# Experts' input: the split parts stored in the order of x, the gather reading every eighth column as its weights

## Chip, cores and metric

The kernel runs on one core of a Trainium2 chip. The metric is the device time of one execution in microseconds (us). Engines are named as in the profile: PE is TensorE's matmul side and PEld its weight loads, DVE is VectorE, ACT is ScalarE, POOL is GpSimd, SP is SyncE, whose queue issues the loads of the weights.

## What is computed

The reference chains a block of two layers (gated linear attention and spatial gating, cross attention to a memory, a mixture of 16 experts) and a second block of one layer (attention and a state space mixer, then again a mixture of 16 experts). All data is float32: 256 tokens of 1024 features. The change lies in the mixture of experts, which thus runs three times. Per layer it is

```python
h = jax.nn.silu(xt @ w_gate[e]) * (xt @ w_up[e])        # for each expert e of 16
y = y + gate[:, e:e + 1] * (h @ w_down[e])              # gate: 2 of the 16 experts per token
```

with `xt` of 256 x 1024, `w_gate[e]` and `w_up[e]` of 1024 x 512, `w_down[e]` of 512 x 1024, so 96 MB of expert weights per layer and 288 MB in all.

## The kernel before

Tokens lie on the partitions in two tiles of 128 (`tt` = 0, 1). In front of each mixture of experts, `before_moe` (line 329) takes the output of the last projection, normalises it and computes the router's logits `lg`. It also prepares the experts' input. `normal` (line 346) scales the rows on ACT into `z`; `high` (line 353) copies `z` on ACT to a tile `xsh` of type float32r, its high part; `low` (line 357) subtracts on DVE and writes the rest to `xsl`. The four views that these steps use come from `views` (line 341). In the trace these are `xsh<-x` (`xsh<-h` in the third layer) at L98, the line of the helper `cp`, and `xsl<-x,xsh` at L78, the line of the helper `tt`.

The order of columns matters here. The expert weights are loaded (line 206) with rows that follow each other on a partition, partition p holding rows 8p to 8p+7, so that a tile of the contraction needs features p*8+k for a fixed k. The kernel before brings the input into that order when it splits it: `high` and `low` read `z` as "p (j k) -> p k j", every eighth element first, 32 bytes apart, and write `xsh` and `xsl` so that feature 8j+k stands at column 128k+j. Tile k is then 128 neighbouring columns.

`moe` (line 848) runs the router, which ends in `sel` and `pos`, the slot of each token at each of its experts. `Dm` (L78) holds ones where a token belongs to a slot, 64 slots per expert. `gather` (line 872) multiplies with it: `lhsT`, the weights that PE loads, is a tile of 128 columns of `xsh` or `xsl`; the moving operand is `Dm` for four experts, 256 columns. For one pair of tiles k that is 2 parts x 2 tiles k x 2 token tiles, 8 weight loads and 8 matmuls; the results go from PSUM to `XG` through ACT and DVE (lines 92, 91, 95). All matmuls are issued in the helper at L64, so that they are told apart by tile names: `gath` is the gather, `gu` the gate and up products, `dn` the down product, `ysum` the sum into the output.

Per layer the first four experts are gathered at once before any expert product, 32 matmuls of `gath`. The further 12 experts come in 12 bursts of 8, two in each of the first six turns of the loop over expert pairs, in the order of the program: gate product, `ysum` of two pairs before, burst, up product, down product of the pair before, burst. So there are 128 `gath` matmuls per layer, 384 in all, and 12 splits of 128 x 1024 (six `high`, six `low`).

The expert weights arrive in loads of 1 MB. Some 17 are issued before the experts begin (`preload`, line 193), into rooms that other stages use otherwise; each further load goes into a room that an earlier one leaves, and SP waits in its queue until the product that reads the earlier one (`gu` or `dn` on PE) is done.

Of the kernel before, what the change touches and what calls it, by code (L numbers as in the profile page):

```python
# [17 lines left out]
KT = D // 128  # L18
# [6 lines left out]
class Net:  # L25
# [303 lines left out]
    def before_moe(self, x, rw, v, mean, keep, got):  # L329

        nc = self.nc
        w, G, B, n = rw
        xs = [self.t8(i, None, F32R) for i in ("xsh", "xsl")]
        lg = self.sm("lg", [128, 40], bufs=1)[:, :2 * n].rearrange("p (t n) -> p t n", t=2)
        mv, q, st, rs, nr = {}, {}, {}, {}, {}

        def views(tt):
            z = x[:, tt, :] if mean else keep[:, tt, :]
            return [z] + [z.rearrange("p (j k) -> p k j", k=KT)] + \
                [i[:, tt, :].rearrange("p (k j) -> p k j", k=KT) for i in xs]

        def normal(tt):
            z = views(tt)[0]
            if mean:
                self.act(z, x[:, tt, :], AF.Identity, scale=rs[tt], bias=nr[tt])
            else:  # L350
                self.act(z, x[:, tt, :], AF.Copy, scale=rs[tt])

        def high(tt):
            _, z, h, _ = views(tt)
            return self.cp(h, z).ins

        def low(tt):
            _, z, h, o = views(tt)
            self.tt(o, z, h.bitcast(F32), OP.subtract)

        def finish(tt):

            self.mul(x[:, tt, :], x[:, tt, :], v[:, 0, :])
            self.add(x[:, tt, :], x[:, tt, :], v[:, 1, :])

        def part(tt, c, A):
            with self.urgent("bm"):
                return steps(tt, c, A)

        def steps(tt, c, A):  # L370
            o = x[:, tt, c * 512:(c + 1) * 512]
            if c == 0:
                st[tt] = self.sm("st", [128, 2, 6])
                q[tt] = self.acc([128, n], "q")
            if mean:
                self.stt(o, o, ALPHA, A, OP.mult, OP.add)
            else:
                self.stt(o, A, 0.5, o, OP.mult, OP.add)
            z = self.s2("zT", [128, 4, 128])
            p = self.rp([128, 4, 128], "trp")  # L380
            for j in range(4):
                kk = 4 * c + j
                nc.tensor.transpose(p[:, j, :], x[:, tt, kk * 128:(kk + 1) * 128], self.ident)
            self.cp(z, p)
            if mean:
                nc.vector.bn_stats(st[tt][:, c, :], o)
            for j in range(4):
                kk = 4 * c + j
                turned = self.mm(q[tt], z[:, j, :], w[:, kk, :], kk == 0, kk == KT - 1).ins
            if c == 0:  # L390
                if tt:
                    normal(0)
                    high(0)
                    low(0)
                return
            rs[tt] = self.sm("rs", [128, 1])
            if mean:
                mv[tt] = self.sm("mv", [128, 2])
                nc.vector.bn_aggr(mv[tt], st[tt])
                self.rsqrt(rs[tt], mv[tt][:, 1:2], 1e-5, near=True)  # L400
            else:
                ss = self.sm("ss", [128, 1])
                self.act(xs[1][:, tt, :], x[:, tt, :], AF.Square, scale=0.03125, accum_out=ss)
                self.rsqrt(rs[tt], ss, 1e-6, near=True)
            p = q[tt]
            if mean:
                g = self.sm("lgt", [128, n])
                self.stt(g, G, mv[tt][:, 0:1], p, OP.mult, OP.add)
                p = g
                nr[tt] = self.sm("nr", [128, 1])  # L410
                self.stt(nr[tt], mv[tt][:, 0:1], -1.0, rs[tt], OP.mult, OP.mult)
            self.stt(lg[:, tt, :], p, rs[tt], B, OP.mult, OP.add)
            if tt == 0:
                return turned
            normal(1)

        def second(exp):
            with self.after(exp):
                h = high(1)
            if exp:  # L420
                with self.after(h):
                    self.warm()
        got.extend((lg, xs, (second, lambda: low(1)), (lambda: [finish(t) for t in range(2)]) if mean else None))
        return part
# [423 lines left out]
    def moe(self, lg, xs, second, finish, gc, route, Wg, Wu, Wd, fill, source):  # L848
# [14 lines left out]
        Dm = self.t8("Dm", [128, 2, 16, 64], F32R)  # L863
# [8 lines left out]
        def gather(e, ks):  # L872

            if e >= NE:
                return
            if e not in XG:
                XG[e] = self.t8("XG", [128, KT, 4, 64])
            with self.urgent("ga"):
                ps = {k: self.rp([128, 2, 4, 64], "gath") for k in ks}
                for i in range(2):  # L880
                    for k, p in ps.items():
                        for kk in (k, k + 1):
                            for tt in range(2):
                                self.mmp(p[:, kk - k], xs[i][:, tt, kk * 128:(kk + 1) * 128], Dm[:, tt, e:e + 4, :],
                                         tt == 0 and i == 0 and kk == k, tt == 1 and i == 1)
                for k, p in ps.items():
                    for kk in (k, k + 1):
                        o, g = XG[e][:, kk], gain[:, kk:kk + 1]
                        b = None if offset is None else offset[:, kk:kk + 1]
                        if kk % 2:  # L890
                            last = self.ts(o, p[:, kk - k], g, b, OP.mult, None if b is None else OP.add)
                        else:
                            self.act(o, p[:, kk - k], AF.Copy if b is None else AF.Identity, scale=g,
                                     **({} if b is None else {"bias": b}))
            return last
# [3 lines left out]
        with self.after(first):  # L899
            second[1]()  # L900
        last = gather(0, (0, 2, 4, 6))
        with self.after(first):
            for e in (4, 8, 12):
# [107 lines left out]
        for i in range(NE // 2):  # L1011
            pg = up(i, 0)
            if i > 1:
                spread(i - 2)
            gather(i // 2 * 4 + 4, (4 * (i % 2),))
            pu = up(i, 1)
            h = middle(pg, pu)
            if i:
                down(i - 1)
            gather(i // 2 * 4 + 4, (4 * (i % 2) + 2,))  # L1020
            if i == 0:
                slot_gates()
            if i == last and over:
                self.tc.keep_in_program_order(
                    nc.vector.tensor_scalar(flag, cm, float(self.cap), None, op0=OP.is_gt))
            rows(i)
            fill(i)
            turned(i, h)
# [515 lines left out]
```

## Time and profile before

| | us |
|---|---|
| median of 3 runs | 1460.03 |
| lowest and highest of them | 1458.52, 3515.89 |
| the profiled execution, its own time | 1460.11 |
| its span, first to last instruction | 1458.3 |
| busy in the span: PE | 1375.7 |
| busy in the span: PEld | 899.7 |
| busy in the span: DVE | 636.3 |
| busy in the span: ACT | 504.8 |

The profile is of one execution. What lies around the span is 1460.11 - 1458.3 = 1.8 us. PEld runs beside PE, so their sum is no time. Matmuls are pipelined: the busy time of one, some 0.28 us for 256 columns, is longer than the step from one to the next, which has to be read from how many fit in a stretch. Times of the three mixtures of experts in the span: 258 to 480 us, 700 to 920 us, 1193 to 1410 us.

### The profile page before, as it was taken

To read this page: it belongs to the slowest core of one execution; us is meant where nothing else is said; L and a number is where in the kernel's file an instruction comes from. 1 tells how busy PE (TensorE), PEld (TensorE's weight loads), DVE (VectorE), ACT (ScalarE), POOL (GpSimd) and SP (SyncE) were. 2 spreads that over 40 slices of the span, in tenths; PEclk is the share of its full clock that TensorE was granted. 3 is DMA by queue.
4 is the path that set the end of the run, shared out by engine and by line. 5 is a ranking of instruction groups with operands and counts; after the bars stand their busy time and mean duration, and the time that the engine had idled before them with its cause. 6 is when DMAs were issued, how large, how long until landed. Compare 5 with 4: busy or idle time off the path is not lost. (4 is left out here: it accounts for less than half of the span.)

```text
span 1458.3 us, 18050 instructions
## 1 busy us (share of the span) xinstructions
PE 1375.7 (94%) x7258; PEld 899.7 (62%) x7258; DVE 636.3 (44%) x1088; ACT 504.8 (35%) x784; POOL 63.7 (4%) x107
## 2 busy tenths in 40 slices
PE   8999999999988898999899998799999979999987
PEld 7889897444433686898444433499878864444335
DVE  5754754412111767654512111657776641212134
ACT  5634443211101474443211101548764440111132
POOL 2110000000000103000000000000000000000000
PEclk9999999999999999999899999899999989999998
DMA  9745557799999965446799999844534679999991
GB/s 341 271 173 173 174 178 267 280 399 421 420 419 420 320 224 175 145 174 243 297 404 380 422 420 420 326 133 134 185 129 137 227 288 378 421 380 420 420 380 44
DMA packets 101964, 421.50 MB, mean 289 GB/s; under 512 B 10676, under 2 KB 10896, under 8 KB 65008
## 3 DMA queue, kind: packets, MB, share of 16 engines
q1 hardware_dynamic: 97968, 409.17, 72.4%
q0 software_dynamic: 3904, 11.09, 2.3%
q8 instruction: 60, 0.98, 0.3%
q14 instruction: 32, 0.26, 0.0%
HBM read 419.18 MB, written 1.05 MB: 288 GB/s over the span
## 5 line engine op out<-in xcount | busy, mean ns | idle before, releaser
L64 PE MATMUL gu<-we,XG 128*64 128x512 f32 x1536 | 347.0, 596 | 4.2 <-DMA we<-in_w_up_dram 1.9
L78 DVE TENSOR_TENSOR whl<-raw,whl 128x1024 fp32r<-128x1024 f32 (+1 forms) x210 | 241.1, 1163 | 144.6 <-ACT whl L98 143.7
L98 ACT ACTIVATE whl<-raw 128x1024 fp32r<-128x1024 f32 (+1 forms) x210 | 208.2, 1009 | 200.8 <-PE acc L64 97.2
L64 PEld LDWEIGHTS gu<-we,XG 128*64 128x64 f32 x1536 | 108.1, 137 | 208.2 <-issue 193.9
L64 PE MATMUL acc<-whl,xTh 128*128 128x512 f32 (+2 forms) x640 | 193.0, 387 | 4.6 <-ACT xTh L98 3.4
L64 PE MATMUL dn<-we,mid 128*64 128x512 f32 x768 | 179.3, 599 | 16.0 <-DMA we<-in_w_down_dram 13.9
L64 PEld LDWEIGHTS dn<-we,mid 128*64 128x64 f32 x768 | 58.0, 138 | 130.2 <-issue 101.6
L64 PEld LDWEIGHTS acc<-whl,xTh 128*128 128x128 f32 x640 | 119.6, 194 | 29.9 <-ACT xTh L98 4.0
L64 PE MATMUL facc<-xTh,whl 128*128 128x256 f32 x640 | 123.8, 289 | 1.7 <-ACT xTh L98 1.7
L64 PE MATMUL acc<-whl,xTl 128*128 128x512 f32 (+1 forms) x320 | 119.8, 385 | 0.2 <-DVE xTl L78 0.2
L95 ACT ACTIVATE dh<-dn,gsl 128x512 fp32r<-128x512 f32 x42 | 28.9, 688 | 258.8 <-PE dn L64 258.8
L78 DVE TENSOR_TENSOR mid<-mid,gu 128x512 f32<-128x512 f32 x24 | 25.3, 1056 | 211.3 <-PE gu L64 138.7
L64 PEld LDWEIGHTS facc<-xTh,whl 128*128 128x128 f32 x640 | 103.2, 195 | 2.4 <-ACT xTh L98 1.9
L64 PE MATMUL facc<-xTl,whl 128*128 128x256 f32 x320 | 91.6, 287 | 0.0
L87 DVE SCALAR_TENSOR_TENSOR dl<-dn,gsl,dh 128x512 fp32r<-128x512 f32 x42 | 31.5, 750 | 127.6 <-ACT dh L95 125.2
L95 ACT ACTIVATE XG<-gath,gc 128x256 f32<-128x256 f32 x48 | 25.3, 535 | 125.8 <-PE gath L64 117.8
L64 PEld LDWEIGHTS acc<-whl,xTl 128*128 128x128 f32 x320 | 60.5, 193 | 12.7 <-issue 0.7
L64 PEld LDWEIGHTS facc<-xTl,whl 128*128 128x128 f32 x320 | 61.9, 193 | 0.5 <-issue 0.3
L92 DVE TENSOR_SCALAR XG<-gath,gc 128x256 f32<-128x256 f32 x32 | 17.1, 543 | 100.6 <-ACT XG L95 100.2
L95 ACT ACTIVATE mid<-gu 128x512 f32<-128x512 f32 x24 | 14.3, 595 | 121.9 <-PE gu L64 115.4
L64 PE MATMUL acc<-whl,oTh 128*128 128x512 f32 x160 | 49.5, 402 | 0.5 <-ACT oTh L98 0.5
L64 PEld LDWEIGHTS gath<-Dm,xsh 128*128 128x128 f32 x192 | 30.7, 221 | 27.0 <-issue 17.1
(366 smaller groups left out, 1759.3 us busy)
## 6 DMA issues: line engine op xcount, KB each, us to landing
we<-in_w_gate_dram SPq DMA_DIRECT2D x96, 1024.0 KB, 12.7
we<-in_w_up_dram SPq DMA_DIRECT2D x96, 1024.0 KB, 11.8
we<-in_w_down_dram SPq DMA_DIRECT2D x96, 1024.0 KB, 16.7
raw<-in_w_in_dram SPq DMA_DIRECT2D x38, 1024.0 KB, 10.2
raw<-in_w_out_dram SPq DMA_DIRECT2D x12, 1024.0 KB, 5.0
raw<-in_wk_x_dram SPq DMA_DIRECT2D x8, 1024.0 KB, 9.1
raw<-in_wv_x_dram SPq DMA_DIRECT2D x8, 1024.0 KB, 5.7
raw<-in_wq_x_dram SPq DMA_DIRECT2D x8, 1024.0 KB, 5.0
```

Source lines behind the costliest of these rows:

```text
L64: return self.nc.tensor.matmul(out, lhsT=l, rhs=r, start=start, stop=stop, skip_group_check=True)
L78: return self.nc.vector.tensor_tensor(out, a, b, op=op)
L87: return self.nc.vector.scalar_tensor_tensor(out, a, s, b, op0=op0, op1=op1, **k)
L92: return self.nc.vector.tensor_scalar(out, a, s1, s2, op0=op0, op1=op1)
L95: return self.nc.scalar.activation(out, a, f, **k)
L98: return self.nc.scalar.activation(out, a, AF.Copy)
```

## The change

`views` hands `high` and `low` plain rows: both read `z` and write `xsh` and `xsl` in the order of the features, contiguous on both sides. The gather picks its tile itself: its weights are now the 128 columns k, k+8, k+16, ..., that is every eighth float32 of a row, 32 bytes apart. The values and the rest of the program are the same. The order of the instructions on PE, ACT, DVE, POOL and SP, with their shapes, is the same in both kernels, row for row; only the access patterns of the 12 splits and of the 384 weight loads differ.

```diff
         def views(tt):
             z = x[:, tt, :] if mean else keep[:, tt, :]
-            return [z] + [z.rearrange("p (j k) -> p k j", k=KT)] + \
-                [i[:, tt, :].rearrange("p (k j) -> p k j", k=KT) for i in xs]
+            return [z, z] + [i[:, tt, :] for i in xs]
...
                             for tt in range(2):
-                                self.mmp(p[:, kk - k], xs[i][:, tt, kk * 128:(kk + 1) * 128], Dm[:, tt, e:e + 4, :],
+                                self.mmp(p[:, kk - k], xs[i][:, tt, :].rearrange("p (j k) -> p k j", k=KT)[:, kk], Dm[:, tt, e:e + 4, :],
                                          tt == 0 and i == 0 and kk == k, tt == 1 and i == 1)
```

## Rows read from the trace of the kernel before

**Rows 1.** Windows: us, length, busy (count) per engine, PEclk, DMA share, GB/s.
```profile
420.00:480.00 60.00, 50.83 (x227) 19.56 (x227) 10.03 (x16) 8.04 (x13) 0.00 (x0) 1.00 1.02 416
880.00:920.00 40.00, 33.36 (x135) 11.61 (x133) 4.46 (x8) 4.02 (x6) 1.05 (x2) 0.96 1.02 416
1360.00:1400.00 40.00, 36.15 (x160) 13.18 (x158) 5.15 (x7) 3.65 (x6) 0.00 (x0) 1.00 1.02 419
```
**Rows 2.** Windows around the pauses of the weight loads, columns as in rows 1.
```profile
306.00:310.00 4.00, 4.00 (x28) 2.40 (x28) 2.67 (x5) 1.65 (x3) 0.00 (x0) 1.00 0.86 313
790.00:796.00 6.00, 6.00 (x32) 2.00 (x30) 1.06 (x1) 0.00 (x0) 0.00 (x0) 1.00 0.50 172
1284.00:1290.00 6.00, 6.00 (x32) 2.00 (x30) 1.06 (x1) 0.00 (x0) 0.00 (x0) 1.00 0.49 167
```
**Rows 3.** Waits of SP's queue from 776 to 800: us in total, times, longest.
```profile
SPq L213 <- PE gu L64: 17.8, 2, 13.0
```
**Rows 4.** Splits: by tile, ns min/median/max; by form, busy us, mean ns, idle before.
```profile
L98 ACT ACTIVATE xsh<-x x4: 2026/2048/2162, 249.1 to 697.1; 128x1024 fp32r<-128x1024 f32 x4
L78 DVE TENSOR_TENSOR xsl<-x,xsh x4: 1991/2018/2034, 251.8 to 700.4; 128x1024 fp32r<-128x1024 f32 x4
...
L78 DVE TENSOR_TENSOR whl<-raw,whl 128x1024 fp32r<-128x1024 f32 x186 | 224.8, 1222 | 136.1 <-ACT whl L98 135.2
L98 ACT ACTIVATE whl<-raw 128x1024 fp32r<-128x1024 f32 x186 | 193.6, 1056 | 179.3 <-PE acc L64 87.4 <-PE facc L64 58.7 <-DMA raw<-in_w_ple_proj_dram 17.0
...
L78 DVE TENSOR_TENSOR whl<-raw,whl 128x528 fp32r<-128x528 f32 x24 | 16.3, 704 | 8.6 <-ACT whl L98 8.4
L98 ACT ACTIVATE whl<-raw 128x528 fp32r<-128x528 f32 x24 | 14.7, 640 | 21.5 <-PE acc L64 9.8 <-PE facc L64 5.9 <-DMA raw<-in_w_in_dram 4.0
```
**Rows 5.** Timeline, first layer, tile 1: start us, us, engine, line [idle before].
```profile
251.79 1.99 DVE L78 TENSOR_TENSOR xsl<-x,xsh 128x1024 fp32r<-128x1024 f32 x1
252.01 2.12 POOL L104 TENSOR_TENSOR rs<-rs,mhalf 128x1 f32<-128x1 f32 x1 [4.43 <-DVE rs L103]
254.17 0.16 DVE L87 SCALAR_TENSOR_TENSOR nr<-mv,rs 128x1 f32<-128x1 f32 x1 [0.39 <-POOL rs L104]
```
**Rows 6.** Timeline, second layer: split of tile 0 and the logits behind it.
```profile
691.92 2.05 ACT L98 ACTIVATE xsh<-x 128x1024 fp32r<-128x1024 f32 x1
694.01 2.00 DVE L78 TENSOR_TENSOR xsl<-x,xsh 128x1024 fp32r<-128x1024 f32 x1 [1.34 <-ACT xsh L98]
695.93 0.22 DVE L87 SCALAR_TENSOR_TENSOR lgt<-gwc,mv,q 128x16 f32<-128x16 f32 x1
```
**Rows 7.** Timeline, third layer: the second high part and the gather that waits.
```profile
1192.66 2.05 ACT L98 ACTIVATE xsh<-h 128x1024 fp32r<-128x1024 f32 x1
...
1194.76 3.33 PE L64 MATMUL gath<-Dm,xsh 128*128 128x256 f32 x15 [0.52 <-ACT xsh L98]
```
**Rows 8.** Weight loads: by tile, ns min/median/max; by form, busy us, mean ns.
```profile
L64 PEld LDWEIGHTS gath<-Dm,xsl x192: 187/192/330, 262.0 to 1345.7; 128*128 128x128 f32 x192
...
L64 PEld LDWEIGHTS gu<-we,XG 128*64 128x64 f32 x1536 | 108.1, 137 | 208.2 <-issue 193.9 <-DMA we<-in_w_gate_dram 5.2 <-DMA we<-in_w_up_dram 5.1
```
**Rows 9.** Timeline, first layer: second half of the first burst.
```profile
272.27 0.64 PE L64 MATMUL gath<-Dm,xsl 128*128 128x256 f32 x4
```
**Rows 10.** Windows of tile gath alone, start of each first gather (PE, PEld, DVE, ACT).
```profile
258.54:262.20 3.66, 3.63 (x16) 3.61 (x17) 0.00 (x0) 0.00 (x0) 0.50 0.16 65
700.25:706.20 5.95, 5.95 (x27) 5.90 (x28) 0.54 (x1) 0.90 (x2) 0.50 0.22 92
1193.65:1197.90 4.25, 3.69 (x16) 3.43 (x17) 0.00 (x0) 0.00 (x0) 0.53 0.69 287
```
**Rows 11.** Windows of tile gath alone, between first gather and pause of the loads.
```profile
264.50:306.00 41.50, 3.97 (x26) 3.35 (x27) 2.74 (x6) 2.19 (x5) 1.00 0.87 345
707.00:793.00 86.00, 8.29 (x56) 7.21 (x56) 4.81 (x10) 4.53 (x9) 1.00 0.92 379
1200.20:1286.00 85.80, 8.31 (x56) 7.25 (x56) 4.24 (x9) 3.64 (x8) 1.00 0.92 380
```

## Prediction

> **What bounds the kernel now.** I read the windows first, stage by stage. In the three mixtures of experts the DMA engines are full to the end: a share of 1.02 at 416 to 419 GB/s, while PE is busy in only 50.83 of 60, 33.36 of 40 and 36.15 of 40 us [rows 1]. So at the end of each layer PE waits for weights, and it has slack there of 9.2, 6.6 and 3.9 us. A mixture of experts therefore ends when its last load lands. When that is, is set by the last pause of the loads, the last time that SP stood for a room that PE had not yet left. The windows with a low DMA share show these pauses: a share of 0.86 over 4 us around 308, then 0.50 and 0.49 over 6 us around 793 and 1287, with PE busy all the time [rows 2]. The waits of SP's queue name the releaser: the product `gu` on PE, up to 13.0 us in one wait [rows 3]. What makes PE late before the pause comes out one for one at the end of the layer; what makes it late afterwards is hidden, until the slack at the end is used up. That is the frame for both parts of the change.
>
> **Part 1, the splits: a gain.** The 12 splits read every eighth element and take about 2.05 us on ACT and 2.02 us on DVE [rows 4]. The same two instructions with contiguous rows of the same length and types are the splits of the projection weights, 1.06 and 1.22 us [rows 4]. I expect these durations: 1.0 us less for each `high`, 0.8 us less for each `low`. Of 12 splits only those in front of the first gather's start count, and the timeline of each layer shows which:
> - First layer: POOL's `rs`, 0.5 to 0.6 us long elsewhere, takes 2.12 us and ends at 254.13, 0.35 us after DVE's `low` ends, and `nr` with the whole router chain follows it [rows 5]. DVE's `low` starts at 251.79 behind other work and is 0.8 us shorter; `rs` follows: gain 0.8.
> - Second layer: `high` on ACT, `low` on DVE right behind it, then `lgt`, the first step of the logits, right behind that [rows 6]. Gain 1.0 + 0.8 = 1.8.
> - Third layer: both `high` follow one another on ACT (the first, as long, starts at 1189.1), and the gather waits for the second one [rows 7]. Gain 2 x 1.0 = 2.0.
>
> Sum 4.6 us. The bounds are 0 (another wait ends last) and 12 times 0.9, some 11 us.
>
> **Part 2, the weights of the gather: a loss.** No row shows a weight load with a step, so I bound it. A contiguous load of 128 columns takes 0.19 us and one of 64 columns 0.137 [rows 8], so a column costs (0.190 - 0.137) / 64 = 0.8 ns and the 128 columns 0.10 us. A matmul of 256 columns needs as much, and both overlap: four `gath` matmuls take 0.64 us, one alone 0.28, so the step is (0.64 - 0.28) / 3 = 0.12 us [rows 9]. Lower bound of the change: nothing. For the other bound I take the engines that do read with this step. DVE's contiguous element costs (1222 - 704) / 496 = 1.04 ns, ACT's (1056 - 640) / 496 = 0.84 ns; the step adds (2018 - 1222) / 1024 = 0.78 and (2048 - 1056) / 1024 = 0.97 ns [rows 4]. So both engines, with different speeds of their own, come out at 1.8 ns per element. That looks like a price of the memory, paid per jump, and not of the engine. At 1.8 ns the load needs 128 x 1.8 = 0.23 us, covers the matmul's 0.10 and becomes the step: 0.12 -> 0.23, +0.11 us per matmul. At the granted clock of 0.50 (1.2 GHz) the step is already 3.66 / 16 = 0.23 and 5.95 / 27 = 0.22 us [rows 10], so there I add 0.02. The value I take is that one, the nearest row in kind (same step, same type, same memory).
>
> The Trainium skill (SBUF — State Buffer, Specifications) says that SBUF works in lines of 16 bytes and that an access pays when it does not hit a line at least twice. With 32 bytes between elements each is alone in its line. The slow splits agree with it; no run here shows it for TensorE, and the page gives no price.
>
> Per layer the first gather (32 matmuls) and 12 bursts of 8 pay:
> - A burst: 8 x 0.11 = 0.88 us; all 12 of a layer 10.6 us.
> - First gather, at half clock for about 16, 27 and 13 of its 32 matmuls [rows 10] (in the third, 13 at that step before the clock rises): 16 x 0.02 + 16 x 0.11 = 2.1 us; 27 x 0.02 + 5 x 0.11 = 1.1; 13 x 0.02 + 19 x 0.11 = 2.4.
> - Net with part 1, before the first `gu`: 2.1 - 0.8 = +1.3; 1.1 - 1.8 = -0.7; 2.4 - 2.0 = +0.4.
>
> **The sum.** Before the last pause lie 26, 56 and 56 `gath` matmuls [rows 11], so 3, 7 and 7 bursts, 2.6, 6.2 and 6.2 us. The shift of the last load is then 1.3 + 2.6 = 3.9; -0.7 + 6.2 = 5.5; 0.4 + 6.2 = 6.6. The other limit is PE itself: the net of the start plus 10.6 minus the slack of rows 1, that is 1.3 + 10.6 - 9.2 = 2.7; -0.7 + 10.6 - 6.6 = 3.3; 0.4 + 10.6 - 3.9 = 7.1. The larger of the two holds: 3.9 + 5.5 + 7.1 = 16.5 us. What follows a mixture of experts (sum, normalisation, transposes) hangs on its end and moves along. The profiled execution took 1460.1 us, as the median did within 0.1, so I forecast 1476.6 us, 1.1% slower. A difference of 2% (29 us) is about what a measurement of this kernel can tell from no change, so this falls under "same".
>
> **Rivals.**
> - *Weight loads do not care about the step.* Then part 1 alone is left, and since both pauses and slack move with the first `gu`: 1460.1 - 4.6 = 1455.5. For it: the load runs beside the matmul on a path of its own, and a column at 0.8 ns is slow enough that a memory with some reserve could follow. Against it: ACT contiguous needs 0.84 ns, the same pace, and yet the step doubles it. This rival is on the other side of zero; it decides as soon as the loads stay below some 0.2 us. In the same direction the Trainium skill (TensorE: Matmul & The Clock Gate, LDWEIGHTS (loading the stationary operand)) gives the duration of a load by its columns alone, 1/1.2 ns each, which agrees with the 0.8 ns here and knows no term for a step.
> - *The step costs engine cycles and not memory time*, so that loads double at half clock too, to 128 x 3.3 = 0.42 us. The half-clock matmuls then pay 0.21 in place of 0.02, (16 + 27 + 13) x 0.19 = 10.6 us more at most: up to 1487. For it: at half clock, contiguous loads do slow down (330 against 187 ns [rows 8]). Against it: the clock rises with time, so fewer matmuls fall into the slow stretch; I count 1485.
> - *The load is far dearer*, some four times (0.43 us at full clock, if it also no longer runs beside the matmul). A burst then costs 8 x 0.31 = 2.5 us, a layer 30 us and 5 to 8 for the first gather; PE becomes the bound: about 30 + 5 - 2 - 7 = 26 per layer, 1538. For it speaks only that nothing here shows such a load.
> - *All is hidden behind the loads.* Only the net at the start is left, about 1 us in sum: 1461. Against it: the slack of rows 1 is smaller than 10.6 in every layer, and two of the pauses lie late.
>
> **Chances.** Forecast 0.57, own range 1469 to 1484. First rival 0.24, second 0.08, third 0.07, hidden 0.04. The range takes in the first rival and the second and leaves out the third: 1453 to 1490, with some 0.03 below and 0.12 above. Faster by over 2% (below 1430.9): no case reaches it, 0.01. Slower by over 2% (above 1489.3): the third, a part of the second and a tail of the forecast, 0.12. Within 2%: 0.87.
>
> **What would show it.** Splits at 1.06 and 1.22 us, `rs` in the first layer near 1.3 us, `gath` loads of about 0.3 us with a step of 0.23 between matmuls of a burst (a burst in 1.9 us in place of 1.1), the pauses near 793 and 1287 some 5 us later relative to the layer's start, and less idle PE in the last 40 us of each layer. The forecast is wrong if the loads stay at 0.19 us (then 1455), or if PE shows no idle time at all at the end of a layer and DMA does (then the loads cost more than I took).

## Result and the profile after

The changed kernel takes 1479.96 us in the median of 4 runs (1476.29 to 1482.21), the kernel before 1461.6 beside it: ratio 1.0127, 95% interval 1.0107 to 1.0146, that is 15.6 to 21.3 us more. One execution of the kernel before took 3515.89 us and is left out of the ratio. A later comparison gave 1478.1 us of 6 runs and 1.0122 (1.0104 to 1.0140). The forecast was 1476.6 us, 16.5 more: the sign is right, and the size is 1 to 2 us short by the differences of the medians (18.4 and 17.6), 4 by the profiles. The profiled execution took 1480.63 us, its span is 1478.8: 20.5 more than before.

**The two parts, by instruction.** The groups by form, of the changed kernel (busy us, mean ns of one, idle before):

```profile
L64 PEld LDWEIGHTS gath<-Dm,xsl 128*128 128x128 f32 x192 | 50.2, 339 | 0.0
L78 DVE TENSOR_TENSOR xsl<-x,xsh 128x1024 fp32r<-128x1024 f32 x4 | 4.9, 1220 | 0.3 <-ACT xsh L98 0.3
L98 ACT ACTIVATE xsh<-x 128x1024 fp32r<-128x1024 f32 x4 | 4.2, 1051 | 0.0
```

The splits stand at 1.05 us (ACT) and 1.22 us (DVE), where they were 2.05 and 2.02 [rows 4]; the weight loads at 0.34 us instead of 0.19 [rows 8]. Here is the first burst in the timeline of the changed kernel, to be laid beside [rows 9] (start us, us):

```profile
272.21 1.25 PE L64 MATMUL gath<-Dm,xsh 128*128 128x256 f32 x4
273.30 1.15 PE L64 MATMUL gath<-Dm,xsl 128*128 128x256 f32 x4
274.37 1.08 PE L64 MATMUL gu<-we,XG 128*64 128x512 f32 x4
```

Four matmuls take 1.15 us where they took 0.64. From start to start of each the step is 0.240 us, against 0.120 before. Behind `gu` or `dn` the first step of a burst grows from 0.22 to 0.35, and such a burst, from the last product in front of it to the first behind it, is 0.97 to 1.02 us longer. Four bursts of each layer (the fifth, seventh, ninth and eleventh) stand behind `ysum`; there the first step stays at 0.12, and they are 0.85 to 0.88 longer. The forecast had 0.88 for all; the 12 bursts of a layer come to 11.3 us, not 10.6. At this step of 8 elements the clock does not change the time from one matmul to the next. Windows of the changed kernel over the first gather of the first layer, its first half at 0.50, its second with the clock risen:

```profile
257.00:261.00 4.00, 3.84 (x15) 3.85 (x16) 3.86 (x10) 0.23 (x1) 0.00 (x0) 0.50 0.34 141
261.00:265.00 4.00, 4.00 (x18) 4.00 (x17) 1.17 (x3) 1.69 (x3) 0.00 (x0) 0.92 0.00 0
```

and its timeline there:

```profile
257.16 4.29 PE L64 MATMUL gath<-Dm,xsh 128*128 128x256 f32 x16 [0.84 <-DVE Dm L78]
261.24 3.97 PE L64 MATMUL gath<-Dm,xsl 128*128 128x256 f32 x16
```

From start to start it is 0.240 us in both halves, but for the first two steps of 0.38 and 0.34 (and two of 0.20 and 0.23 as the clock rises). Before, it was 0.213 in the half at 0.50 and 0.118 to 0.120 at full clock.

**What the shorter splits release.** First layer, tile 1, timeline of the changed kernel, answering to [rows 5]:

```profile
251.09 1.22 DVE L78 TENSOR_TENSOR xsl<-x,xsh 128x1024 fp32r<-128x1024 f32 x1
251.32 1.40 POOL L104 TENSOR_TENSOR rs<-rs,mhalf 128x1 f32<-128x1 f32 x1 [4.43 <-DVE rs L103]
...
252.75 0.16 DVE L87 SCALAR_TENSOR_TENSOR nr<-mv,rs 128x1 f32<-128x1 f32 x1 [0.44 <-POOL rs L104]
```

POOL's `rs` begins 0.22 to 0.23 us behind the start of DVE's `xsl` in both kernels, and ends 0.41 us after it here (252.72 against 252.31), 0.35 before: 2.12 us became 1.40 without any change to POOL's instruction. In the third layer the gather waits for the second high part as before, which is now 1.04 us long; its wait is down to 0.23 us [rows 7]:

```profile
1205.43 3.99 PE L64 MATMUL gath<-Dm,xsh 128*128 128x256 f32 x15 [0.23 <-ACT xsh L98]
```

**The loads and the slack.** Windows of the changed kernel, columns as in rows 1: first the pauses, then the ends of the layers.

```profile
306.00:310.00 4.00, 4.00 (x22) 1.41 (x20) 0.00 (x0) 0.00 (x0) 0.00 (x0) 1.00 1.00 420
310.00:314.00 4.00, 4.00 (x24) 3.02 (x22) 1.98 (x3) 1.99 (x4) 0.00 (x0) 1.00 0.61 188
796.00:804.00 8.00, 8.00 (x38) 2.90 (x40) 1.02 (x2) 0.56 (x1) 0.00 (x0) 1.00 0.18 72
1302.00:1308.00 6.00, 6.00 (x30) 2.01 (x28) 0.37 (x1) 0.00 (x0) 0.00 (x0) 1.00 0.03 11
430.00:470.00 40.00, 40.00 (x184) 14.83 (x182) 4.49 (x6) 3.17 (x5) 0.00 (x0) 1.00 1.01 419
890.00:930.00 40.00, 36.30 (x154) 13.12 (x152) 6.12 (x11) 5.48 (x9) 1.05 (x2) 0.96 1.02 415
1370.00:1410.00 40.00, 39.88 (x188) 17.03 (x190) 6.97 (x11) 5.41 (x9) 0.00 (x0) 1.00 1.01 420
```

The pauses of [rows 2] are later and deeper (a share of 0.18 over 8 us around 800, 0.03 over 6 us around 1305). SP still waits for `gu`, up to 13.9 us in one wait where it was 13.0 [rows 3]. And the idle PE time in these windows [rows 1] has shrunk: none in the first layer, 3.7 us in the second, 0.1 in the third. What PE still waits for to the end of the first layer (400 to 486 us: us in total, times, longest) was before:

```profile
PE dn L64 <- DMA we<-in_w_down_dram: 5.3, 4, 1.3
PE gu L64 <- DMA we<-in_w_up_dram: 1.9, 1, 1.9
PE gu L64 <- DMA we<-in_w_gate_dram: 0.8, 1, 0.8
PE dn L64 <- ACT mid L98: 0.7, 1, 0.7
PE trp L450 <- DVE DT L91: 0.4, 1, 0.4
```

and is in the changed kernel:

```profile
PE dn L64 <- ACT mid L98: 0.7, 1, 0.7
PE trp L449 <- DVE DT L91: 0.4, 1, 0.4
```

No wait for a load is left: here PE itself has become the limit. In the third layer the full window is not the whole story, for behind it PE still waits for a load:

```profile
1419.33 1.94 PE L64 MATMUL dn<-we,mid 128*64 128x512 f32 x8 [1.35 <-DMA we<-in_w_down_dram]
```

The page says the same in its groups for the expert products (busy us, mean ns, idle before), first of the kernel before:

```profile
L64 PE MATMUL gu<-we,XG 128*64 128x512 f32 x1536 | 347.0, 596 | 4.2 <-DMA we<-in_w_up_dram 1.9 <-DMA we<-in_w_gate_dram 1.9 <-DVE XG L92 0.2
...
L64 PE MATMUL dn<-we,mid 128*64 128x512 f32 x768 | 179.3, 599 | 16.0 <-DMA we<-in_w_down_dram 13.9 <-ACT mid L98 2.1
```

and of the changed one:

```profile
L64 PE MATMUL gu<-we,XG 128*64 128x512 f32 x1536 | 343.8, 601 | 0.1
...
L64 PE MATMUL dn<-we,mid 128*64 128x512 f32 x768 | 176.0, 598 | 6.5 <-DMA we<-in_w_down_dram 4.4 <-ACT mid L98 2.1
```

PE stood idle in front of these products for 20.2 us before and for 6.6 now: 13.6 of the 34 us that the 36 bursts add went into idle time.

**One thing that was not in the forecast.** Behind the second burst of each layer the granted clock falls to 0.50 (1.2 GHz). Timeline of the changed kernel, PE, first layer, from the start of the second burst to that of the third:

```profile
281.39 1.25 PE L64 MATMUL gath<-Dm,xsh 128*128 128x256 f32 x4
...
283.46 1.84 PE L64 MATMUL pg<-gparts,Dm 128*128 128x4 f32 x16
285.16 0.82 PE L75 MATMUL dtp<-ident,pos 128*128 128x128 f32 x4
285.77 1.06 PE L75 MATMUL gut<-ident,mid 128*128 128x128 f32 x4
286.76 8.14 PE L64 MATMUL gu<-we,XG 128*64 128x512 f32 x32
294.83 1.24 PE L64 MATMUL gath<-Dm,xsh 128*128 128x256 f32 x4
```

The same stretch of the kernel before:

```profile
279.85 0.74 PE L64 MATMUL gath<-Dm,xsh 128*128 128x256 f32 x4
...
283.63 7.09 PE L64 MATMUL gu<-we,XG 128*64 128x512 f32 x32
290.65 0.74 PE L64 MATMUL gath<-Dm,xsh 128*128 128x256 f32 x4
```

and the windows of the changed kernel in the three layers:

```profile
286.00:288.00 2.00, 2.00 (x8) 0.96 (x9) 1.04 (x3) 0.60 (x1) 0.00 (x0) 0.50 0.92 385
730.00:732.00 2.00, 2.00 (x9) 1.02 (x9) 1.04 (x3) 0.60 (x1) 0.00 (x0) 0.50 0.96 401
1236.00:1238.00 2.00, 2.00 (x6) 0.48 (x4) 0.00 (x0) 0.00 (x0) 0.00 (x0) 0.54 0.13 53
```

Between the starts of the second and third burst lie 2.65 us more than before, not 1.0, so the fall costs some 1.65 us there. PE was not idle ahead of it: it did the burst, and then 16 `pg` matmuls of four columns, each behind a weight load.

**Ledger.** For each layer, the time from the start of the first `gu` to that of the last `ysum` in each kernel's profiled execution; a star marks a layer in which the clock fell behind one of its first two bursts.

| us | layer 1 | layer 2 | layer 3 |
|---|---|---|---|
| before | 220.9 | 219.7 | 220.7 |
| splits alone | 220.6 | 219.6 | 220.7 |
| changed | 223.0* | 228.1* | 229.1* |
| changed, second profile | 222.5 | 229.5* | 227.4 |
| gather alone | 223.1* | 226.1 | 230.6* |
| changed, `pg` ahead of the up product | 224.2* | 226.5 | 228.9* |
| changed, `pg` apart from bursts | 221.4 | 226.9 | 227.6 |
| the same, second profile | 221.6 | 226.7 | 227.5 |

Changed against before: layers +2.2, +8.4, +8.5, start of the first `gu` +0.5, stages between the layers -0.6 and +2.5 (in the second of them the clock falls at 1067 and 1101 in the changed kernel's profile and not in that of before, which in turn has a longer fall at 928 to 941; what these are worth is not shown), behind the last `ysum` -0.9: 20.5 in sum.

### The profile page after: what moved, and what is told of

It reads as the page before. It is cut to its first block, busy times and chain, and to the rows that moved or that the text cites. A ratio compares the mean times of both kernels' runs of the same rounds, so it can differ in the third digit from the quotient of the medians.

```text
span 1478.8 us, 18050 instructions
## 1 busy us (share of the span) xinstructions
PE 1413.9 (96%) x7258; PEld 939.4 (64%) x7258; DVE 631.9 (43%) x1088; ACT 498.8 (34%) x784; POOL 62.6 (4%) x107
## 3 DMA queue, kind: packets, MB, share of 16 engines
HBM read 419.18 MB, written 1.05 MB: 284 GB/s over the span
## 5 line engine op out<-in xcount | busy, mean ns | idle before, releaser
L64 PE MATMUL dn<-we,mid 128*64 128x512 f32 x768 | 176.0, 598 | 6.5 <-DMA we<-in_w_down_dram 4.4
L64 PEld LDWEIGHTS gath<-Dm,xsh 128*128 128x128 f32 x192 | 49.4, 332 | 24.3 <-issue 16.2
L64 PE MATMUL gath<-Dm,xsh 128*128 128x256 f32 x192 | 55.0, 424 | 3.8 <-DVE Dm L78 3.6
```

What stands on the lines that cost most here:

```text
L64: return self.nc.tensor.matmul(out, lhsT=l, rhs=r, start=start, stop=stop, skip_group_check=True)
```

## Experiments

**Each part alone.** Splits alone: the changed kernel with the weights of the gather read as before.

```diff
-xs[i][:, tt, :].rearrange("p (j k) -> p k j", k=KT)[:, kk]
+xs[i][:, tt, kk * 128:(kk + 1) * 128]
```

> Part 1 alone: the splits are contiguous as in the changed kernel, the gather loads 128 neighbouring columns as before, so the features that it gathers are in another order than the rows of the expert weights; the threshold of the fallback is raised so that its loop can't start. Theory (the two parts are independent; the loss is the weight loads, the gain is the splits): 4 to 5 us faster than before, about 1456.5; first gu about 0.8, 1.8 and 2.0 us earlier after the start of the router's stage in the three layers; weight loads of the gather at 0.19 us; no fall of the clock behind the second burst. Rival (part of the changed kernel's gain on the path was only apparent, another wait ends last): no change, 1460 to 1461.

Measured: 1453.83 us, ratio 0.995 (0.9933 to 0.9967), 4.8 to 9.8 us faster. The gain is there and rather larger than the 4.6 of the forecast. The profiled execution, the slowest of the four, is 4.3 us shorter. Counted from the router's first matmul (`q`), the first gather starts 0.7, 1.8 and 1.7 us earlier in the three layers, as forecast but for 0.3 in the third. At the first `gu`, where 0.8, 1.8 and 2.0 were expected, only 0.0, 2.2 and 1.0 are left; the remaining 1.1 us lie outside these stages. What is lost or won behind the gather's start goes with the clock: by their steps some 25, 20 and 25 of its 32 matmuls run at half clock, where it was 17, 27 and 14. In the first layer the last 16 take 2.93 us against 2.15.

Gather alone: the kernel before with the gather's line of the change, so with the diff above the other way round.

> Part 2 alone: the splits are strided as before, and the gather takes every eighth column, so again the features are in another order than the expert weights; fallback threshold raised. Theory: the changed kernel without its gain, 1480 + 4.5 = 1484.5 us, some 23 us over before; a step of 0.24 us between gather matmuls and weight loads of 0.34 us; the clock falls behind the second burst in each layer. Rival (the strided loads cost less, the changed kernel lost elsewhere): 1470 or below.

Measured: 1482.29 us, ratio 1.0155 (1.0138 to 1.0171), 20 to 25 us slower. The clock falls behind the second burst in the first and third layer, not in each as expected. So the loss is all in the strided weights; by the medians the splits give back some 4 of it (1.0155 - 1.0127 of 1461 us), about what the forecast had put for them.

**Same loads, other place.** The kernel before, with strided weights for one group of four experts only, the last (bursts 9 to 12) or the second (bursts 1 to 4): 96 strided loads in both.

```diff
-xs[i][:, tt, kk * 128:(kk + 1) * 128]
+(xs[i][:, tt, :].rearrange("p (j k) -> p k j", k=KT)[:, kk] if e == 12 else xs[i][:, tt, kk * 128:(kk + 1) * 128])
```

> Splits as before; only the gather of the last four experts (bursts 9 to 12 of each layer, behind the last pause of the weight loads) takes every eighth column, 32 of 128 matmuls per layer; features of these experts in another order, fallback threshold raised. Theory (what makes PE late behind the last pause is hidden by the loads up to the slack at the end, 9.2, 6.6 and 3.9 us): 4 x 0.98 = 3.9 us more of PE per layer, all or nearly all hidden: 1460 to 1463, within 0.2% of before. Rival (PE is the bound and each us counts wherever it lies): 3 x 3.9 = 11.8 us slower, 1473.

> Splits as before; only the gather of experts 4 to 7 (bursts 1 to 4 of each layer, ahead of the last pause) takes every eighth column, again 32 matmuls per layer; features of these experts in another order, fallback threshold raised. Theory: 3.9 us per layer lie ahead of the pause and come out at the end of the layer (3 us in the first layer), and the clock falls behind the second burst and adds up to 1.7 us per layer: 11 to 16 us slower, 1472 to 1477. Rival that all PE time is hidden by the loads: 1461. Rival that place does not matter: the same time as with the last four experts.

Measured: late 1461.65 us, ratio 1.0007 (0.9995 to 1.002); early 1474.74 us, ratio 1.007 (1.0037 to 1.0103). Twelve late bursts cost nothing measurable, twelve early ones 5 to 15 us. The five early runs spread from 1466 to 1476 us, and the profile is of the one at 1474.74. The windows show why early and late differ. Late bursts:

```profile
790.00:796.00 6.00, 6.00 (x30) 2.01 (x28) 1.06 (x1) 0.00 (x0) 0.00 (x0) 1.00 0.49 165
1360.00:1400.00 40.00, 37.75 (x176) 14.56 (x173) 5.22 (x8) 4.12 (x6) 0.00 (x0) 1.00 1.01 418
```

Early ones:

```profile
790.00:796.00 6.00, 6.00 (x32) 3.42 (x30) 0.54 (x1) 1.16 (x2) 0.00 (x0) 1.00 1.01 419
796.00:802.00 6.00, 6.00 (x30) 2.01 (x28) 0.43 (x1) 0.00 (x0) 0.00 (x0) 1.00 0.34 139
```

With the late bursts the pause stands where it stood [rows 2] and only slack is eaten: 37.75 busy of 40 us against 36.15 [rows 1]. With the early ones the pause itself is 6 us later. By the ledger's measure the layers with late bursts take 220.7, 219.5 and 220.7 us, as before. With the early ones the third layer is 3.8 us longer, for four bursts of 1.0, and the second 7.1, with a fall of the clock behind its second burst. So the mechanism of the forecast is shown for the second and third layer: what makes PE late before the last pause counts, what comes behind it is hidden up to the slack. It fails in the first layer: three of the four bursts lie ahead of its pause, 3 us, and the layer is 0.6 us longer (221.5), with PE still waiting for loads. Why the loads make up the rest there is open.

**What is paid for.** The changed kernel with steps of 2, 3, 4 and 16 elements for the weights of the four groups of experts.

```diff
-xs[i][:, tt, :].rearrange("p (j k) -> p k j", k=KT)[:, kk]
+(lambda s, f: f[:, :128 * s].rearrange("p (j k) -> p k j", k=s)[:, kk % s])((2, 3, 4, 16)[e // 4], xs[i].rearrange("p t d -> p (t d)"))
```

> The changed kernel with another step between the columns that the gather loads: 2 elements (8 bytes) for experts 0 to 3, 3 (12 bytes) for 4 to 7, 4 (16 bytes) for 8 to 11, 16 (64 bytes) for 12 to 15; the gathered features are then not the ones that the product needs, fallback threshold raised. Read in the trace are the weight loads and the step between gather matmuls at full clock. Theory (price per line of 16 bytes that a load touches, about 1.8 ns a line): step 2 touches 64 lines and stays at 0.12 us; step 3 touches 96 lines and comes to some 0.18; step 4 touches 128 lines, 0.24, and step 16 the same 0.24. Rival (price per jump, whatever its length): 0.24 us for all four. Rival (price grows with the distance): 16 dearer than 4.

One profiled execution, 1468.44 us. Third layer of its timeline, the second half of a burst at step 3, at step 4 and at step 16:

```profile
1232.82 0.87 PE L64 MATMUL gath<-Dm,xsl 128*128 128x256 f32 x4
...
1275.75 1.11 PE L64 MATMUL gath<-Dm,xsl 128*128 128x256 f32 x4
...
1330.97 1.04 PE L64 MATMUL gath<-Dm,xsl 128*128 128x256 f32 x4
```

From start to start a matmul takes 0.12 us at step 2 (at full clock, in the first gather), 0.175 at step 3, 0.235 at step 4, 0.240 at step 8 (the changed kernel) and 0.222 at step 16. (The first step of a burst is left aside.) The price neither grows with the distance nor falls on each jump alike. It follows the number of 16-byte pieces that 128 float32 at that step touch: 64, 96, 128, 128, 128. 0.175 / 96 and 0.235 / 128 are both 1.8 ns, and 64 of them are 0.117 us, hidden behind the matmul. Step 16 is a little cheaper than that, by 6%, for which no run gives a reason. The Trainium skill (SBUF — State Buffer, Specifications) speaks of 16-byte lines that want two hits each for full bandwidth; the trace agrees, with step 2 free and step 4 at the full price. The rule that a weight load takes its columns by 1/1.2 ns (the Trainium skill, TensorE: Matmul & The Clock Gate, LDWEIGHTS (loading the stationary operand)) would leave the step at 0.12 us for every one of these; the trace disagrees from step 3 on, and the measurement decides.

**Contiguous splits and a cheap gather together.** If step 2 is free, rows of `w_gate` and `w_up` loaded in pairs let the gather read every second column of 256. Each packet of these loads is then 4 KB instead of 8 KB. From the kernel before, beside the contiguous splits and the order of one small constant:

```diff
+        if w < 2:
+            self.tc.keep_in_program_order(self.nc.sync.dma_start(
+                raw.rearrange("p (g k) f -> p g (k f)", k=2),
+                W[w][e].rearrange("(g p k) f -> p g (k f)", g=4, k=2)[:, 2 * h:2 * h + 2, :]))
+            return raw
...
-xs[i][:, tt, kk * 128:(kk + 1) * 128]
+xs[i][:, tt, kk // 2 * 256:kk // 2 * 256 + 256].rearrange("p (j k) -> p k j", k=2)[:, kk % 2]
```

> The changed kernel with another split of the features over partitions: rows of the gate and up weights come in pairs (partition p holds rows 256g+2p and 256g+2p+1 for g of 0 to 3), in packets of 4 KB in place of 8 KB, and the gather takes every second column of a block of 256. Nothing is left out. Theory (with 8 bytes between columns two of them share a line and the load costs no more than a contiguous one; the splits stay contiguous): the gain of the contiguous splits alone, 5 to 7 us faster than before, 1454 to 1456, if packets of 4 KB run at the same 420 GB/s. Rivals: step 2 costs too, then 1470 or more; packets of 4 KB run slower, then each per cent of rate on the 64 MB of gate and up weights per layer costs some 1.6 us a layer, 5 us in all.

Measured: 1466.03 us, ratio 1.0032 (1.002 to 1.0044): slower, though loads of the gather are at 0.195 us and the splits at 1.05 and 1.22. The page's line on packets and a window:

```profile
DMA packets 126540, 421.50 MB, mean 288 GB/s; under 512 B 10676, under 2 KB 10896, under 8 KB 114160
```
```profile
300.00:420.00 120.00, 120.00 (x596) 50.73 (x592) 22.56 (x34) 17.75 (x29) 2.25 (x3) 1.00 1.02 411
```

The same stretch of the kernel before:

```profile
300.00:420.00 120.00, 120.00 (x595) 51.47 (x592) 22.12 (x34) 17.73 (x29) 1.85 (x3) 1.00 1.01 416
```

At a full DMA share the rate is 411 against 416 GB/s, 1.2% less (404 against 409 from 750 to 880 us). The rival named in the expectation holds in kind: a kernel bound by its loads pays, by estimate, 1.2% of some 220 us in each of three layers, about 8 us. In the ledger's measure the layers take 222.1, 222.0 and 222.6 us, 5.8 more than with the splits alone, whose profile is 10.6 us shorter. The other 4.8 us lie in the stages around the layers, and their cause is open, as is whether the rate goes with the size of the packets or with the order in which the rows are read.

**The fall of the clock.** Two kernels move the 16 `pg` matmuls of the changed one; the first puts them behind the first burst, ahead of the up product:

```diff
+            if i == 0:
+                slot_gates()
...
-            if i == 0:
-                slot_gates()
```

> The changed kernel with one thing moved: the 16 small matmuls pg of each layer come behind the first burst and ahead of the up product, no longer right behind the second burst. Theory (the granted clock falls to half after burst, pg and transposes in a row, in which PE's columns stream slowly): no fall of the clock some 21 us behind the first gather in any layer, up to 5 us less than the changed kernel, 1475 to 1478. Rival (the fall follows from the longer bursts alone): it stays, 1480.

Measured: 1482.69 us, ratio 1.0143 (1.0116 to 1.0171), no gain. In the profile the clock falls at 277.1 in the first layer and at 1226.0 in the third, now behind the first burst: the fall went along with `pg`. The second kernel puts them into the second turn, between its up and its down product, with no burst next to them:

```diff
+            if i == 1:
+                slot_gates()
...
-            if i == 0:
-                slot_gates()
```

> The changed kernel, with the 16 small matmuls pg (4 columns each) moved from behind the second burst into the second turn, between the up product and the down product, away from any burst. Theory: the granted clock fell behind the second burst because burst and pg matmuls, both held up by their weight loads, followed each other; apart, no layer shows the clock at 0.5 there, and up to 1.7 us per layer come back: 1475 to 1478 us instead of 1480. Rival: the bursts alone do it; the clock falls behind a burst as before and the time stays at 1480.

Measured: 1479.73 us, ratio 1.0123 (1.0102 to 1.0143). The clock stays up behind every burst, and the `gu` behind the second one has its 7.09 us back:

```profile
285.12 7.09 PE L64 MATMUL gu<-we,XG 128*64 128x512 f32 x32
```

Its layers are 1.6, 1.2 and 1.5 us shorter than those of the changed kernel (ledger), but the time is the same. Between the first and the second layer it takes 225.9 us, and the changed kernel 220.9; in that mixer, where PE has pauses, the clock is at half in the one and full in the other. Window of the kernel with `pg` apart:

```profile
580.00:584.00 4.00, 3.34 (x15) 3.34 (x16) 1.40 (x5) 0.22 (x1) 0.02 (x1) 0.50 0.00 0
```

of the changed kernel:

```profile
580.00:584.00 4.00, 3.18 (x22) 2.27 (x21) 3.22 (x11) 0.81 (x2) 1.54 (x3) 1.00 0.00 0
```

Whether each of these falls was an accident of one execution was asked with both kernels once more, on one chip:

> The changed kernel once more, beside the next run on the same chip and with more executions. Theory: 1480 us as before, the clock at 0.5 behind the second burst in at least two of the three layers of the profiled execution. Rival: the falls behind the second burst were an accident of one profiled execution; none is seen here, at the same time of 1480.

> The changed kernel with the pg matmuls away from the bursts, once more with more executions. Theory: no fall of the clock behind a burst, each layer from its first gather to its last sum 1.3 to 1.5 us shorter than in the changed kernel, and, the clock in the stages between being what it happens to be, a median 2 to 5 us below that of the changed kernel on the same chip. Rival: what is saved at the bursts is lost in the stages between (a fall of the clock in the second layer's mixer, 13.7 us long in the first profile of this kernel); the medians are the same within 1 us.

Measured: changed 1478.1 us (1475.07 to 1481.15), `pg` apart 1481.3 us (1478.16 to 1481.86). In the changed kernel the clock now falls behind the second burst of the second layer alone, one layer and not the two or three that were expected. So the fall comes again (and a layer with it is 0.5 to 3.4 us longer than one without, by the ledger), but not in every execution and layer. With `pg` apart there is none at the bursts, and again a fall at 577 us, with 225.8 us from layer to layer. The expectation missed on both counts: the layers are 0.9 and 2.8 us shorter and 0.1 longer, and the median is not 2 to 5 us lower but 3.2 higher, with intervals of the ratio that overlap (1.0104 to 1.0140 and 1.0118 to 1.0156). The rival is right in kind, what is saved at the bursts is lost in between. Why the clock falls in that mixer is open; this order of `pg` is not needed for it, since profiles of the splits alone (578 to 584 us) and of the kernel with the pairs (582 to 585) show a fall there too.

Taken over all profiles: where the first two bursts have weights at a step of 3 or 8 and `pg` stands right behind one of them, the clock fell in 11 of 18 layers. With such bursts and `pg` apart it fell in none of 6, and with `pg` behind a burst whose loads take 0.19 us (contiguous, or at a step of 2) in none of 18. So the fall goes along with both together; why it comes in some layers and not in others is not shown.

**Faster than both.** The gather reads the high parts first and the low parts last, yet DVE makes the low part of tile 0 early. The kernel before, with that part taken from in front of tile 1's statistics on DVE to behind the first half of the slots:

```diff
-                    low(0)
...
-        got.extend((lg, xs, (second, lambda: low(1)), (lambda: [finish(t) for t in range(2)]) if mean else None))
+        got.extend((lg, xs, (second, lambda: [low(t) for t in range(2)]), (lambda: [finish(t) for t in range(2)]) if mean else None))
```

> The kernel before, with the strided subtraction of token tile 0 on DVE moved behind the first half of the slots, next to that of tile 1, so that it no longer stands ahead of the logits. Theory (2 us of DVE lie on the router's path in the first two layers and are free behind it): 1.2 us less in the first layer, 2 us in the second, about nothing in the third, 3 us in all: 1458. Rival (the second half of the gather then waits for the two subtractions, which lie in a row): no change or up to 2 us slower.

Measured: 1458.89 us of 10 runs, ratio 0.9979 (0.9965 to 0.9993): 3 us faster than before (1 to 5), with the strided splits kept. The first gather starts at 257.27, 698.00 and 1191.52 where it was 258.57, 700.25 and 1193.68. But the profile is only 1.1 us shorter, and at the first `gu`, counted from `q`, only the second layer has gained: 1.6 us, against 0.4 us lost in the first and nothing in the third. Where the rest of the 3 us lies is not shown. One step on, for the third layer:

```diff
+            if not mean:
+                return self.act(h, x[:, tt, :].rearrange("p (j k) -> p k j", k=KT), AF.Copy, scale=rs[tt]).ins
...
```

> The kernel before with the low part of tile 0 taken from in front of tile 1's statistics to behind the first half of the slots (as in the run with the late low parts), and in the third layer the high parts copied by ACT straight from x with the scale (same strided read), the normalised rows h written after each. Theory: the third layer's first gather waits for the second high part, which then stands one ACT instruction earlier; its gather starts 1 to 2 us earlier and the time is 1457 to 1458 us. Rival: DVE's low part or the slots end last there instead; the time is that of the run with the late low parts, 1459 us.

Measured: 1459.25 us, ratio 0.9979 (0.9967 to 0.9991): the rival's number. The third layer's timeline shows where the earlier high part goes:

```profile
1188.45 3.57 PE L64 MATMUL gath<-Dm,xsh 128*128 128x256 f32 x15 [0.83 <-ACT xsh L95]
...
1192.99 3.57 PE L64 MATMUL gath<-Dm,xsl 128*128 128x256 f32 x15 [0.75 <-DVE xsl L78]
```

The gather starts 1.0 us earlier than in the run with the late low parts, counted from `q`, but the first `gu` 0.2 us later. The wait for `xsh` is down from 2.30 us in the run with the late low parts to 0.83, but a wait for DVE's second `xsl` is new, and all 32 matmuls run at half clock, 3.57 us for 15, where the clock rose within the gather in the run before it (2.07 us for its last 16).

## Why the prediction was right, step by step

- **Splits, durations.** 1.06 and 1.22 us foretold from the splits of the projection weights, 1.05 and 1.22 measured.
- **Splits, gain.** 4.6 foretold, 4.8 to 9.8 measured alone and some 4 beside the strided gather. The choice of the path in each layer (POOL's `rs`, DVE's `lgt`, ACT's second high part) held: at the start of the gather 0.7, 1.8 and 1.7 us are gained. What the splits alone lose of it behind that, in the first and third layer, goes to half clock.
- **Price of the strided load.** 128 x 1.8 ns = 0.23 us foretold from ACT and DVE, a step of 0.240 measured. "A price of the memory, paid per jump" is half right: the runs show it per 16-byte piece touched. At step 8 both are the same number.
- **Half clock.** 0.02 us more per matmul foretold, 0.213 to 0.240 measured, 0.03 (the forecast's 0.23 and 0.22 of before had the two long first steps in them). The second rival, engine cycles, would have needed 0.42 us there (0.46, if its 1.8 ns is really doubled) and falls; the first rival (1455.5) falls with the loads at 0.34 us, the third (four times dearer) with the same row, and the fourth (all hidden) with the difference between early and late bursts.
- **Bursts.** +0.88 us each foretold, +0.97 to 1.02 measured in eight of a layer's 12 and +0.85 to 0.88 in the four behind `ysum`. The term that was mis-sized is "8 x 0.11": a step grows by 0.12, and eight of them are 0.97; in the four, the first step does not grow. Per layer 11.3 us, against 10.6.
- **First gather.** Net +1.3, -0.7, +0.4 at the first `gu`, counted from the start of the router's stage; measured +1.2, -0.6, +0.35 in the profile after.
- **Pauses and slack.** From the first `gu` on the sum gave 2.6, 6.2 and 6.7 us. The layers without a fall of the clock show +0.6 to 1.7, +6.4 to 7.2 and +6.7 to 6.9 (gather alone, second profile, `pg` ahead and `pg` apart). In the second layer the pause holds: its 7 bursts come to 6.7. In the third the sum took the limit of PE itself, and that choice was wrong: PE still waits 1.3 us for a load at the end, with `pg` apart as in the changed kernel, so the pause holds there too, 6.7 again. In the first the sum took the pause, 3.9 in place of 2.7, and that was wrong as well: "one for one" fails there (0.6 us for three early bursts), and in four of six profiles with strided weights throughout no wait for a load is left. The other limit, 1.4 from the first `gu` on, comes nearer.
- **What was missing.** Falls of the clock behind the bursts: the layers of the changed kernel's profile take 19.0 us more, against 15.5 foretold and 14.5 and 14.7 measured with `pg` apart, so they are worth some 4 us there. Where they come varies between executions. The difference between the forecast and the medians, 1.5 to 3.4 us, is of this size; that it is this cause is argued and not shown, since the kernel without falls at the bursts was no faster.
- **Luck.** The price of the load, the path of the splits and the pause of the second layer were reasoned and came out. That the total came within 1 to 2 us of the measured difference is in part luck: the first layer was put 1 to 2 us too high, the bursts too low, and the falls of the clock and the stages between the layers were not in the sum.

## What to carry to other kernels

A layout that one part of a kernel wants has to be paid once, and the place decides: twelve splits before the product cost some 4 to 7 us on engines that are partly free, the same step in 384 weight loads cost some 22 on the engine that the loads of the experts wait for. A price for an access that no row shows can be taken from other engines that read the same memory in the same pattern. And a delay has to be placed against the last pause of the loads: 96 slow weight loads cost nothing behind it and 5 to 15 us ahead of it. How much of a delay gets through has to be measured for each stage: in two layers it was all of it, in the first 0.6 of 3 us.

## What the hardware did that was not expected

- Weight loads with 128 float32 columns are free at a step of 2 elements (0.12 us between matmuls) and cost their full price at 4 and beyond (0.235, 0.240, 0.222 us at steps 4, 8, 16). At step 8 it is 0.240 at both levels of the clock.
- The granted clock fell to 0.50 with PE busy without a gap, behind a burst with strided weights followed by 16 matmuls of four columns; with both it fell in 11 of 18 layers, without `pg` behind a burst in none of 6, and without strided weights in none of 18.
- POOL's small `rs` takes 2.12 us beside a DVE subtraction of 1.99 us with two inputs, 1.40 beside one of 1.22, and 0.54 alone.
- A stretch of the loads, with two thirds of them in packets of 4 KB, ran at 411 GB/s where packets of 8 KB gave 416 (404 against 409 in another).
